# Issuing the combinations of a tile of weights behind the last low part of the tile two ahead of it

## The chip, the cores and the metric

The kernel runs on one core of a Trainium2 chip. What counts is the device time of one execution in microseconds. Times of this kernel are told as the median of several runs, and a profile is one execution of its own, taken by the hardware profiler.

## The reference

One layer of a hybrid block on 512 positions of width 2048, in float32. All of it hangs on large products with weights: one input projection of 22,592 columns, two branch projections and an output projection.

```python
h = rmsnorm(x, norm1_w[l])
proj = jnp.einsum('bsd,de->bse', h, w_in[l])
q, k, v, g_ret, z, xbc, dt_raw, gate_r, gate_s = jnp.split(proj, offsets, axis=-1)
y_r = (retention(q, k, v, positions) * jax.nn.silu(g_ret)).astype(x.dtype)
y_s = ssd(xbc, dt_raw, conv_w[l], conv_b[l], dt_bias[l], a_log[l], d_skip[l])
y_s = rmsnorm((y_s * jax.nn.silu(z)).astype(x.dtype), ssd_norm_w[l])
p_r = jnp.einsum('bse,ed->bsd', y_r, w_br_ret[l])
p_s = jnp.einsum('bse,ed->bsd', y_s, w_br_ssd[l])
merged = jax.nn.sigmoid(gate_r) * p_r + jax.nn.sigmoid(gate_s) * p_s
x = x + jnp.einsum('bsd,de->bse', merged, w_out[l])
return rmsnorm(x, norm_f_w)
```

`retention` has 8 heads of 256 with rotary q and k and a recurrence over chunks of 64; `ssd` is a causal depthwise convolution with a chunked scan over 64 heads in 8 groups. The second branch is 4096 wide, so its projection has twice the rows of the others.

## The kernel before

**The products.** A *unit* computes 256 output columns for all 512 positions: a contraction over 2048 rows in eight steps k of 256 rows. Each step is a 2 x 2 block product (two halves of 128 weight rows and columns, two halves of 256 positions). Most units do it with seven block products in place of eight, by Strassen's scheme (table `SEVEN`); some, called plain, do it with the four weight blocks against all 512 positions (`FOUR`). Float32 accuracy comes from splitting each operand into a high part, rounded to the type that TensorE takes, and a low part, what is left: each block product is three matmuls (high x high, high x low, low x high: lines 221 to 223), so a step is 7 x 3 = 21 matmuls of 256 columns.

**A tile of weights** (`wf`) holds two steps. SP loads it in two DMAs (four where a unit takes its columns from two places). For a Strassen unit VectorE (DVE) then adds the *combinations*, three instructions (lines 238, 240 and 241). Then, for each of the two steps, ScalarE (ACT) casts the seven blocks to the high part `whi` (line 148) and DVE subtracts it from them to make the low part `wlo` (line 149). There are three `wf` buffers, seven of `whi` and six of `wlo`, so the load of a tile waits until the last low part of the tile three back has been made.

**PSUM.** A unit's seven sums go to four buffers, pb0 to pb3 (halves of 256 positions). When they are complete, ACT copies pb0 (line 274) and DVE adds up pb1 (275), pb2 (276 and 277) and pb3 (278) into `o`. In the rotary heads and the SSD groups every unit uses the same four buffers, so the next unit's products can write pb2 only after line 277; in the branch and output projections units alternate between these and the four `att` buffers. The last three steps of a unit (`LAST`) run table group by table group, so that pb0 and pb1 are complete first.

**The stages.** Eight retention heads; eight SSD groups (each with units for B and C, x, z and the gates, and between them the convolution, the decays and the scan); the projection of the retention branch; that of the SSD branch in two halves of 2048 rows, called here the second and third branch projection; the output projection. Between these four the normalized activations are loaded (tiles `r`) and split: a difference, high and low part (lines 173, 174, 176) for the first four operands, and, while the first unit runs, three more (lines 182 to 187). In the third branch projection each unit also loads three tiles `f` a row block, multiplies and adds them (lines 737 on POOL, 738 to 740 on DVE), and stores the result for the output projection to load.

**What sets the order.** No order is written out, but for start and end. A scheduler simulates the program on a model of the engines and lists each engine's instructions; what is ready and has the higher priority goes first, and loads, combinations and parts have a raised priority (`tc.high_priority(offset=PRIO)`). Each engine then works through its list in order, and so does SP's queue of DMAs. `tc.add_manual_dep` with the class `NoSync` tells the scheduler that one instruction must stand behind another on its engine; it adds no semaphore.

## Time and profile before

| | us |
|---|---|
| median of 3 runs (lowest, highest) | 2753.27 (2751.96, 2756.13) |
| the profiled execution, its own time | 2755.9 |
| its span, first to last instruction | 2754.0 |
| TensorE busy | 2691.5 |
| VectorE busy | 2368.3 |
| ScalarE busy | 1342.7 |

The mean granted TensorE clock of that execution is 0.993 of full speed. In the views, PE is TensorE's matmuls, PEld its weight loads (which overlap them), DVE VectorE, ACT ScalarE, POOL GpSimd, SP the engine that issues most DMAs; L149 is line 149. A row of the waits reads: the engine that waited and the line of the instruction, what ended the wait, total us, times, the longest. A row of the time line: start, duration, engine, line, operation, tiles, and in brackets the idle time ahead of it and what ended it. A row of the windows: the stretch, its length, busy time of PE, PEld, DVE, ACT and POOL with the number of instructions, the granted clock, the share of the DMA engines, GB/s. The grouped rows: line, engine, operation, tiles, shapes, count, then busy us and mean ns, then idle time ahead and what ended it.

### The profile page before, as it was taken

To read this page: it belongs to the slowest core of one execution; us is meant where nothing else is said; L and a number is where in the kernel's file an instruction comes from. 1 tells how busy PE (TensorE), PEld (TensorE's weight loads), DVE (VectorE), ACT (ScalarE), POOL (GpSimd) and SP (SyncE) were. 2 spreads that over 40 slices of the span, in tenths; PEclk is the share of its full clock that TensorE was granted. 3 is DMA by queue.
4 is the path that set the end of the run, shared out by engine and by line. 5 is a ranking of instruction groups with operands and counts; after the bars stand their busy time and mean duration, and the time that the engine had idled before them with its cause. 6 is when DMAs were issued, how large, how long until landed. Compare 5 with 4: busy or idle time off the path is not lost.

```text
span 2754.0 us, 51975 instructions
## 1 busy us (share of the span) xinstructions
PE 2691.5 (98%) x20448; PEld 2565.0 (93%) x20448; DVE 2368.3 (86%) x3799; ACT 1342.7 (49%) x1923; POOL 179.3 (7%) x130
## 2 busy tenths in 40 slices
PE   7999999999999999999999999999999999999998
PEld 4899999999999999999999999999999999898897
DVE  7998888888869898888989898898989897898997
ACT  4434333433345555565565555566564353433443
POOL 0000000000000000000000000000000000011221
PEclk9999999999999999999999999999999999999999
DMA  4223333333333444343444434343464644557534
GB/s 156 85 89 108 100 104 104 104 93 104 104 113 121 129 129 129 107 129 114 131 127 134 138 107 125 119 136 121 129 202 154 212 140 131 176 182 226 193 120 138
DMA packets 339766, 362.46 MB, mean 132 GB/s; under 512 B 25152, under 2 KB 297792, under 8 KB 339520
## 3 DMA queue, kind: packets, MB, share of 16 engines
q1 hardware_dynamic: 319136, 325.05, 38.2%
q10 hardware_dynamic: 20384, 34.09, 3.3%
q8 instruction: 160, 2.62, 0.4%
q14 instruction: 86, 0.70, 0.1%
HBM read 321.56 MB, written 37.49 MB: 130 GB/s over the span
## 4 chain that ended last, share of the span: by engine, by line
PE 78%; DVE 9%; DMA 6%; issue 3%; ACT 1%; SPq 1%; POOL 0%; DVEq 0%; ACTq 0%; POOLq 0%
PE pb L223 21%; PE pb L221 21%; PE pb L222 21%; DMA wf<-in_w_in_dram 3%; DVE wlo L149 3%; PE att L222 2%; PE att L223 2%; PE att L221 2%; PE att L545 1%; DVE wf L238 1%; PE att L560 1%; PE att L677 1%; DMA wf<-in_w_br_ssd_dram 1%; PE att L681 1%; PE pb L118 1%
## 5 line engine op out<-in xcount | busy, mean ns | idle before, releaser
L148 ACT CAST whi<-wf 128x896 fp32r<-128x896 f32 (+1 forms) x968 | 817.6, 884 | 908.2 <-PE pb L222 370.4
L149 DVE TENSOR_TENSOR wlo<-wf,whi 128x896 fp32r<-128x896 f32 (+1 forms) x968 | 988.3, 1033 | 57.2 <-ACT whi L148 35.6
L221 PE MATMUL pb<-a,whi 128*128 128x256 f32 (+1 forms) x3328 | 998.3, 303 | 7.7 <-DVE o L277 4.3
L223 PE MATMUL pb<-a,wlo 128*128 128x256 f32 (+1 forms) x3328 | 994.5, 301 | 7.2 <-DVE wlo L149 7.1
L222 PE MATMUL pb<-a,whi 128*128 128x256 f32 (+1 forms) x3328 | 996.8, 300 | 0.0
L221 PEld LDWEIGHTS pb<-a,whi 128*128 128x128 f32 x3328 | 636.0, 191 | 32.3 <-issue 7.4
L223 PEld LDWEIGHTS pb<-a,wlo 128*128 128x128 f32 x3328 | 635.2, 191 | 30.4 <-DVE wlo L149 8.9
L222 PEld LDWEIGHTS pb<-a,whi 128*128 128x128 f32 x3328 | 637.1, 191 | 20.3 <-issue 0.2
L221 PE MATMUL pb<-b,whi 128*128 128x256 f32 x2112 | 600.1, 284 | 0.0
L223 PE MATMUL pb<-b,wlo 128*128 128x256 f32 x2112 | 599.0, 284 | 0.0
L222 PE MATMUL pb<-b,whi 128*128 128x256 f32 x2112 | 598.1, 284 | 0.0
L238 DVE TENSOR_TENSOR wf<-wf 128x512 f32<-128x512 f32 x400 | 286.1, 715 | 173.9 <-DMA wf<-in_w_in_dram 133.0
L221 PEld LDWEIGHTS pb<-b,whi 128*128 128x128 f32 x2112 | 405.8, 192 | 0.1
L222 PEld LDWEIGHTS pb<-b,whi 128*128 128x128 f32 x2112 | 405.8, 192 | 0.0
L223 PEld LDWEIGHTS pb<-b,wlo 128*128 128x128 f32 x2112 | 405.5, 192 | 0.2
L241 DVE TENSOR_TENSOR wf<-wf 128x256 f32<-128x256 f32 x400 | 174.9, 437 | 3.2
L240 DVE TENSOR_TENSOR wf<-wf 128x256 f32<-128x256 f32 x400 | 174.3, 436 | 3.5
L223 PE MATMUL att<-a,wlo 128*128 128x256 f32 (+1 forms) x480 | 144.5, 306 | 5.1 <-DVE wlo L149 5.1
L221 PE MATMUL att<-a,whi 128*128 128x256 f32 (+1 forms) x480 | 145.2, 305 | 0.0
L222 PE MATMUL att<-a,whi 128*128 128x256 f32 (+1 forms) x480 | 145.2, 305 | 0.0
L223 PEld LDWEIGHTS att<-a,wlo 128*128 128x128 f32 x480 | 90.8, 192 | 10.3 <-DVE wlo L149 6.5
L221 PEld LDWEIGHTS att<-a,whi 128*128 128x128 f32 x480 | 92.0, 192 | 3.9
(217 smaller groups left out, 2731.5 us busy)
## 6 DMA issues: line engine op xcount, KB each, us to landing
wf<-in_w_in_dram SPq DMA_DIRECT2D x640, 256.0 KB, 3.1
wf<-in_w_br_ssd_dram SPq DMA_DIRECT2D x128, 256.0 KB, 3.3
wf<-in_w_out_dram SPq DMA_DIRECT2D x72, 256.0 KB, 3.1
wf<-in_w_in_dram SPq DMA_DIRECT2D x128, 128.0 KB, 2.6
L<-A_d SPq DMA_DIRECT2D x32, 512.0 KB, 3.7
wf<-in_w_br_ret_dram SPq DMA_DIRECT2D x64, 256.0 KB, 3.4
ys_d<-B ACTq DMA_DIRECT2D x32, 256.0 KB, 2.0
r<-ys_d SPq DMA_DIRECT2D x16, 512.0 KB, 6.6
```

Source lines behind the costliest of these rows:

```text
L118: ins = getattr(self.engine, name)(*args, **kw).ins
L148: ACT.copy(dst_hi, src)
L149: DVE.tensor_tensor(dst_lo, src, dst_hi.bitcast(F32), op=ALU.subtract)
L221: PE.matmul(o, wh, xh, start=b not in started, stop=False, skip_group_check=True)
L222: PE.matmul(o, wh, xl, start=False, stop=False, skip_group_check=True)
L223: PE.matmul(o, wl, xh, start=False, stop=(k == NP - 1), skip_group_check=True)
L238: DVE.tensor_tensor(f2[:, :, 4:6, :], f2[:, :, 1:3, :], f2[:, :, 0:1, :].to_broadcast([P, 2, 2, P]), op=ALU.subtract)
L240: DVE.tensor_tensor(f2[:, :, 0, :], f2[:, :, 2, :], f2[:, :, 4, :], op=ALU.add)
L241: DVE.tensor_tensor(f2[:, :, 6, :], f2[:, :, 3, :], f2[:, :, 0, :], op=ALU.subtract)
L545: PE.matmul(ps[:, :n], k[:, i, sb * P:(sb + 1) * P], q[:, i, sb * P:], start=(i == 0), stop=(i == 1))
L560: PE.matmul(ps[:, :DK], pt[sb][:, (lb - sb) * P:(lb - sb + 1) * P], v[:, sb, :], start=(sb == 0), stop=(sb == lb))
L677: PE.matmul(pi[i * 64:(i + 1) * 64, c * P:(c + 1) * P], xd[:, c, i, :], L[:, i, c, :], start=True, stop=True)
```

## The change

`split` returns the name of the subtraction that makes the low part, and `products` keeps these names in a list. When the combinations of a tile are written, the first of them is told to stand, on DVE, behind the third-last name: the second low part of the tile two ahead of it. Plain units have no combinations and are unchanged, though their low parts are in the list.

```diff
--- before.py
+++ after.py
@@ -146,7 +146,16 @@
 
     def split(dst_hi, dst_lo, src):
         ACT.copy(dst_hi, src)
-        DVE.tensor_tensor(dst_lo, src, dst_hi.bitcast(F32), op=ALU.subtract)
+        return DVE.tensor_tensor(dst_lo, src, dst_hi.bitcast(F32), op=ALU.subtract).ins.name
+
+    lows = []
+
+    def behind(ins, other):
+
+        tc.add_manual_dep(
+            ins, other,
+            mybir.DependencyInfo(mybir.DependencyClass.NoSync, mybir.DependencyReason.DATA),
+            reason="order of issue")
 
 
 
@@ -235,14 +244,17 @@
                             SP.dma_start(out=v[:, :, c:c + w], in_=rows(ap, k + m))
                             c += w
                     if not plain:
-                        DVE.tensor_tensor(f2[:, :, 4:6, :], f2[:, :, 1:3, :],
-                                          f2[:, :, 0:1, :].to_broadcast([P, 2, 2, P]), op=ALU.subtract)
+                        first = DVE.tensor_tensor(f2[:, :, 4:6, :], f2[:, :, 1:3, :],
+                                                  f2[:, :, 0:1, :].to_broadcast([P, 2, 2, P]), op=ALU.subtract)
+
+                        if len(lows) > 2:
+                            behind(first.ins, lows[-3])
                         DVE.tensor_tensor(f2[:, :, 0, :], f2[:, :, 2, :], f2[:, :, 4, :], op=ALU.add)
                         DVE.tensor_tensor(f2[:, :, 6, :], f2[:, :, 3, :], f2[:, :, 0, :], op=ALU.subtract)
                 f = f2[:, k % 2]
                 hi = wp.tile([P, 7, P], F32R, name="whi", bufs=HB)
                 lo = wp.tile([P, 7, P], F32R, name="wlo", bufs=LB)
-                split(hi[:, :n, :], lo[:, :n, :], f[:, :n, :])
+                lows.append(split(hi[:, :n, :], lo[:, :n, :], f[:, :n, :]))
             ws.append((hi, lo))
             if k < NP - LAST:
                 for g in groups:
```

The lines behind the first new one move by 9 and, behind the second, by 12: lines 221 to 223 become 230 to 232, 238, 240, 241 become 247, 252, 253, and 275 to 278 become 287 to 290.

Since the scheduler simulates the whole program, the orders of DVE, PE, ACT and SP change in many places. On DVE the same instructions stand in another order. Before, the first combination of 199 of the 400 tiles with combinations stood ahead of the last low part of the tile two back; after the change, of none. On ACT, 13 loads of an activation table at line 672 are gone.

**Place 1: the end of a unit in an SSD group, on DVE** (`wf_13224`, `wf_13280`, `wf_13315` are three tiles in a row, each with two low parts, of which those of `wf_13224` are `wlo_13231` and `wlo_13256`; `o_13148` is the unit whose sums are added up). Before:

```order
L149 TENSOR_TENSOR wlo_13231<-wf_13224,whi_13230 128x896
L240 TENSOR_TENSOR wf_13280<-wf_13280 128x2x128
L241 TENSOR_TENSOR wf_13280<-wf_13280 128x2x128
L238 TENSOR_TENSOR wf_13315<-wf_13315 128x2x256
L275 TENSOR_TENSOR o_13148<-pb1_12921,o_13148 128x512
L240 TENSOR_TENSOR wf_13315<-wf_13315 128x2x128
L241 TENSOR_TENSOR wf_13315<-wf_13315 128x2x128
L276 TENSOR_TENSOR o_13148<-o_13148,pb2_12922 128x2x256
L149 TENSOR_TENSOR wlo_13256<-wf_13224,whi_13255 128x896
L277 TENSOR_TENSOR o_13148<-o_13148,pb2_12922 128x256
L149 TENSOR_TENSOR wlo_13287<-wf_13280,whi_13286 128x896
L278 TENSOR_TENSOR o_13148<-pb3_12923,o_13148 128x2x256
```

and now:

```order
L252 TENSOR_TENSOR wf_13280<-wf_13280 128x2x128
L253 TENSOR_TENSOR wf_13280<-wf_13280 128x2x128
L287 TENSOR_TENSOR o_13148<-pb1_12921,o_13148 128x512
L149 TENSOR_TENSOR wlo_13231<-wf_13224,whi_13230 128x896
L288 TENSOR_TENSOR o_13148<-o_13148,pb2_12922 128x2x256
L149 TENSOR_TENSOR wlo_13256<-wf_13224,whi_13255 128x896
L247 TENSOR_TENSOR wf_13315<-wf_13315 128x2x256
L289 TENSOR_TENSOR o_13148<-o_13148,pb2_12922 128x256
L149 TENSOR_TENSOR wlo_13287<-wf_13280,whi_13286 128x896
L149 TENSOR_TENSOR wlo_13312<-wf_13280,whi_13311 128x896
L252 TENSOR_TENSOR wf_13315<-wf_13315 128x2x128
L290 TENSOR_TENSOR o_13148<-pb3_12923,o_13148 128x2x256
```

The first combination of `wf_13315` stood ahead of all four sums and of `wlo_13256`; it now stands behind both low parts of `wf_13224`. The first sum (275, now 287) no longer has `wlo_13231` ahead of it, and the last one (278, now 290) has `wlo_13312` ahead of it as well.

On PE, the start of the unit that follows (pb2 is the buffer that line 277 frees). Before, and now:

```order
L223 MATMUL pb0_13164<-a2_211,wlo_13231 128x256
L221 MATMUL pb1_13165<-a2_211,whi_13230 128x256
L221 MATMUL pb2_13166<-a0_200,whi_13174 128x256
L222 MATMUL pb2_13166<-a0_200,whi_13174 128x256
L223 MATMUL pb2_13166<-a0_200,wlo_13175 128x256
```

```order
L232 MATMUL pb0_13164<-a2_211,wlo_13231 128x256
L230 MATMUL pb1_13165<-a2_211,whi_13230 128x256
L231 MATMUL pb1_13165<-a2_211,whi_13230 128x256
L232 MATMUL pb1_13165<-a2_211,wlo_13231 128x256
L230 MATMUL pb1_13165<-b2_429,whi_13230 128x256
L231 MATMUL pb1_13165<-b2_429,whi_13230 128x256
L232 MATMUL pb1_13165<-b2_429,wlo_13231 128x256
L230 MATMUL pb2_13166<-a0_200,whi_13174 128x256
```

The third step's products for pb1 now all stand ahead of the first product for pb2, five matmuls more. The first product for pb3 comes as the 55th matmul of the unit in place of the 37th.

**Place 2: the seventh unit of the third branch projection, on DVE** (`wf_28433` and `wf_28468` are its last two tiles with their low parts `wlo_28440`, `wlo_28465` and `wlo_28475`, `wlo_28479`; `r0`, `r1` and so on are the operands loaded for the output projection). Before:

```order
L278 TENSOR_TENSOR o_28289<-att_28064,o_28289 128x2x256
L173 TENSOR_TENSOR r0_28743<-r0_28743 128x256
L241 TENSOR_TENSOR wf_28468<-wf_28468 128x2x128
L738 TENSOR_TENSOR f_28295<-f_28295,o_28289 128x512
L738 TENSOR_TENSOR f_28306<-f_28306,o_28289 128x512
L149 TENSOR_TENSOR wlo_28440<-wf_28433,whi_28439 128x896
L149 TENSOR_TENSOR wlo_28465<-wf_28433,whi_28464 128x896
L739 TENSOR_TENSOR f_28295<-f_28295,f_28297 128x512
L149 TENSOR_TENSOR wlo_28475<-wf_28468,whi_28474 128x896
L173 TENSOR_TENSOR r1_28749<-r1_28749 128x256
L149 TENSOR_TENSOR wlo_28479<-wf_28468,whi_28478 128x896
```

and now, in two pieces that follow each other:

```order
L247 TENSOR_TENSOR wf_28468<-wf_28468 128x2x256
L149 TENSOR_TENSOR wlo_28440<-wf_28433,whi_28439 128x896
L182 TENSOR_TENSOR r0_28743<-r0_28743 128x256
L750 TENSOR_TENSOR f_28295<-f_28295,o_28289 128x512
L149 TENSOR_TENSOR wlo_28465<-wf_28433,whi_28464 128x896
L750 TENSOR_TENSOR f_28306<-f_28306,o_28289 128x512
L252 TENSOR_TENSOR wf_28468<-wf_28468 128x2x128
```

```order
L182 TENSOR_TENSOR r1_28749<-r1_28749 128x256
L751 TENSOR_TENSOR f_28295<-f_28295,f_28297 128x512
L182 TENSOR_TENSOR r2_28755<-r2_28755 128x256
L253 TENSOR_TENSOR wf_28468<-wf_28468 128x2x128
L752 TENSOR_TENSOR f_28295<-f_28295,f_28299 128x512
L182 TENSOR_TENSOR r3_28761<-r3_28761 128x256
L149 TENSOR_TENSOR wlo_28475<-wf_28468,whi_28474 128x896
L149 TENSOR_TENSOR wlo_28479<-wf_28468,whi_28478 128x896
```

`wlo_28440` stands ahead of the difference on r0 where it stood behind; those on r1, r2 and r3 stand ahead of both low parts of `wf_28468`, where only r1 stood ahead of the second.

**Place 3: the start of the output projection, on DVE** (`wf_29008`, `wf_29064`, `wf_29120` are the first three tiles with combinations; `wlo_29015` is the first low part of the first). Before, and now:

```order
L238 TENSOR_TENSOR wf_29120<-wf_29120 128x2x256
L173 TENSOR_TENSOR r7_28573<-r7_28573 128x256
L182 TENSOR_TENSOR xo5_28801<-r0_28743 128x512
L182 TENSOR_TENSOR xo6_28802<-r1_28749 128x512
L241 TENSOR_TENSOR wf_29064<-wf_29064 128x2x128
L240 TENSOR_TENSOR wf_29120<-wf_29120 128x2x128
L149 TENSOR_TENSOR wlo_29015<-wf_29008,whi_29014 128x896
```

```order
L253 TENSOR_TENSOR wf_29008<-wf_29008 128x2x128
L182 TENSOR_TENSOR r7_28573<-r7_28573 128x256
L191 TENSOR_TENSOR xo5_28801<-r0_28743 128x512
L191 TENSOR_TENSOR xo6_28802<-r1_28749 128x512
L253 TENSOR_TENSOR wf_29064<-wf_29064 128x2x128
L192 TENSOR_TENSOR xo5_28801<-r0_28743,xo5_28801 128x256
L149 TENSOR_TENSOR wlo_29015<-wf_29008,whi_29014 128x896
L192 TENSOR_TENSOR xo6_28802<-r1_28749,xo6_28802 128x256
L149 TENSOR_TENSOR wlo_29040<-wf_29008,whi_29039 128x896
L247 TENSOR_TENSOR wf_29120<-wf_29120 128x2x256
L185 TENSOR_TENSOR a7_28785<-r7_28573,a7_28785 128x1024
L149 TENSOR_TENSOR wlo_29071<-wf_29064,whi_29070 128x896
```

The combinations of `wf_29120` began ahead of that low part; they now begin behind both low parts of `wf_29008`.

## Prediction

> **What bounds the kernel now.** I read the page first, then the windows, then who waited for whom, then the time line at the worst places. The head of the page and its chain of waits:
>
> ```profile
> span 2754.0 us, 51975 instructions
> PE 2691.5 (98%) x20448; PEld 2565.0 (93%) x20448; DVE 2368.3 (86%) x3799; ACT 1342.7 (49%) x1923; POOL 179.3 (7%) x130
> PE 78%; DVE 9%; DMA 6%; issue 3%; ACT 1%; SPq 1%; POOL 0%; DVEq 0%; ACTq 0%; POOLq 0%
> ```
>
> TensorE stands idle for only 2754.0 - 2691.5 = 62.5 us, so no edit on VectorE can bring more than that, and what the change can bring lies in the part of it for which TensorE waits on VectorE. The windows show where it lies (rotary heads, SSD groups, first two branch projections, third branch projection, start of the output projection):
>
> ```profile
> 120.00:790.00 670.00, 667.05 (x5283) 649.39 (x5282) 569.42 (x993) 255.13 (x330) 22.57 (x30) 1.00 0.33 101
> 790.00:2080.00 1290.00, 1277.74 (x9961) 1224.22 (x9960) 1117.76 (x1760) 752.58 (x1151) 87.63 (x65) 1.00 0.42 129
> 2080.00:2390.00 310.00, 310.00 (x2295) 297.00 (x2295) 259.98 (x403) 130.54 (x169) 2.05 (x1) 1.00 0.51 168
> 2390.00:2545.00 155.00, 144.09 (x1088) 138.52 (x1088) 140.01 (x213) 54.73 (x72) 18.32 (x11) 0.98 0.60 193
> 2585.00:2612.00 27.00, 22.53 (x148) 21.20 (x149) 27.00 (x43) 13.90 (x19) 10.36 (x1) 0.87 0.39 132
> ```
>
> The columns are length, then busy time of PE, PEld, DVE, ACT and POOL. From 120 to 790 and from 2080 to 2390 TensorE loses 3 us and nothing. The loss sits in the SSD groups (12.3 us of 1290), the third branch projection (10.9 of 155) and the first units of the output projection (4.5 of 27). In the last two VectorE is busy 90% and 100%: there it is the bound, with TensorE waiting for it. Who ended TensorE's waits in these three windows, in that order:
>
> ```profile
> PE pb L221 <- DVE o L277: 4.3, 6, 1.7
> PE att L677 <- issue: 2.9, 3, 1.4
> PE pb L221 <- DVE o L275: 0.7, 2, 0.5
> ...
> PE pb L223 <- DVE wlo L149: 5.7, 3, 4.1
> PE att L223 <- DVE wlo L149: 5.1, 6, 1.9
> ...
> PE att L222 <- DVE b L187: 1.9, 1, 1.9
> PE att L221 <- ACT b L185: 1.7, 2, 1.1
> PE pb L223 <- DVE wlo L149: 0.9, 1, 0.9
> ```
>
> VectorE itself stands still for weights, over the whole run, at the first combination (line 238):
>
> ```profile
> DVE wf L238 <- DMA wf<-in_w_in_dram: 133.0, 157, 2.9
> DVE wf L238 <- DMA wf<-in_w_br_ssd_dram: 25.9, 21, 2.0
> ```
>
> That is 159 us in 178 waits, 0.89 us each, and nearly all of it costs nothing today: TensorE's waits for VectorE in the rows above are 18.6 us.
>
> **The change, part by part.** No instruction is added or taken away on DVE, PE, SP or POOL; the combinations move. Durations for what moves:
>
> ```profile
> L149 DVE TENSOR_TENSOR wlo<-wf,whi 128x896 fp32r<-128x896 f32 x800 | 872.2, 1100 | 46.7 <-ACT whi L148 31.8 <-PE pb L223 11.9 <-ACT yn L570 0.9
> L238 DVE TENSOR_TENSOR wf<-wf 128x512 f32<-128x512 f32 x400 | 286.1, 715 | 173.9 <-DMA wf<-in_w_in_dram 133.0 <-DMA wf<-in_w_br_ssd_dram 25.9 <-DMA wf<-in_w_br_ret_dram 8.4
> L240 DVE TENSOR_TENSOR wf<-wf 128x256 f32<-128x256 f32 x400 | 174.3, 436 | 3.5
> L241 DVE TENSOR_TENSOR wf<-wf 128x256 f32<-128x256 f32 x400 | 174.9, 437 | 3.2
> ```
>
> A tile of weights has three combinations (0.715 + 0.436 + 0.437 = 1.59 us) and two low parts (2.20 us). In the order before, the combinations of every second tile stand ahead of the last low part of the tile two back; now all stand behind it. A tile's load may start when the last low part of the tile three back has been made, so the move puts up to 2.20 us of other work between the start of that load and the instruction that needs it. Against the mean wait of 0.89 us this removes most of VectorE's waits. What it is worth goes stage by stage.
>
> *SSD groups (790 to 2080).* The unit at 1188 us, whose order stands in the part on the change:
>
> ```profile
> 1188.99 0.69 DVE L238 TENSOR_TENSOR wf<-wf 128x512 f32<-128x512 f32 x1 [0.97 <-DMA wf<-in_w_in_dram]
> 1191.69 0.69 DVE L238 TENSOR_TENSOR wf<-wf 128x512 f32<-128x512 f32 x1 [0.21 <-DMA wf<-in_w_in_dram]
> 1195.30 0.41 DVE L277 TENSOR_TENSOR o<-o,pb 128x256 f32<-128x256 f32 x1
> 1195.85 0.36 PE L221 MATMUL pb<-a,whi 128*128 128x256 f32 x1 [0.16 <-DVE o L277]
> ```
>
> Two waits for weights (1.18 us) stand ahead of the sums that free PSUM, and TensorE waits at their end. In the new order one low part (1.10) and one first combination (0.72) leave the place ahead of the first sum (L275): 1.8 us earlier. L277 has two third-size combinations less ahead of it (0.87 us earlier), and L278 has one low part and one combination more (1.10 + 0.44 - 0.87 = 0.67 us later). On PE the products that need pb2 stand 5 matmuls later and those that need pb3 18 later; at 0.12 us from start to start (14 matmuls in the PE rows below: 1.56 / 13) 0.6 and 2.2 us. So L277 gains 1.5 us against its user and L278 too (2.2 - 0.7). The other groups have this unit in the same order, so the waits on L277 and L275 (4.3 + 0.7) should go: I take 4 of the 5 us. From below: nothing, if VectorE, now earlier, only waits for TensorE's sums; from above 5.0 + 2.9, with the wait at line 677, which follows work on ACT and VectorE that comes earlier too.
>
> *Third branch projection (2390 to 2545).* VectorE's own waits there, and the worst place:
>
> ```profile
> DVE wf L238 <- DMA wf<-in_w_br_ssd_dram: 8.0, 8, 1.9
> DVE f L739 <- POOL f L737: 4.1, 3, 1.7
> DVE r L173 <- DMA r<-mm_d: 2.5, 1, 2.5
> ...
> 2524.26 0.28 PE L221 MATMUL pb<-a,whi 128*128 128x256 f32 x1
> 2525.82 0.28 PE L222 MATMUL pb<-a,whi 128*128 128x256 f32 x1
> 2530.24 0.80 PE L223 MATMUL pb<-a,wlo 128*128 128x256 f32 x2 [4.13 <-DVE wlo L149]
> ...
> 2531.00:2533.00 2.00, 2.00 (x12) 2.00 (x11) 2.00 (x4) 0.00 (x0) 0.00 (x0) 0.50 0.63 200
> 2533.00:2535.00 2.00, 2.00 (x11) 2.00 (x11) 2.00 (x4) 0.62 (x1) 0.00 (x0) 0.50 0.68 186
> ```
>
> VectorE's waits (14.6 us) and TensorE's (5.7 + 5.1 = 10.8) are two sides of one thing here. After the stall of 4.13 us the granted clock is 0.50 for two windows: 23 matmuls in 4 us, against 33 at 0.12 us; 10 x 0.12 = 1.2 us more. So 12 us can be won. The change moves two low parts ahead of the load of r that held up the wait of 4.13 us: one of the two that TensorE needs (wlo_28440) no longer stands behind the 2.5 us. But the loads of weights in this stage are late for another reason too:
>
> ```profile
> SPq L704 <- DMA mm_d<-f: 29.8, 11, 5.7
> 2516.10 0.42 SPq L704 DMA_DIRECT2D f<-m_d  x1
> 2522.33 0.34 SPq L704 DMA_DIRECT2D f<-ps_d  x1
> 2522.76 0.39 SPq L205 DMA_DIRECT2D r<-mm_d  x1
> 2524.26 1.44 SPq L205 DMA_DIRECT2D r<-mm_d  x3
> ```
>
> SP, in order, holds the loads of weights behind a load of f that waits for a store, up to 5.7 us, and no move of combinations shortens that. So I take half of the 8.0 us, 4 us, and leave the clock's 1.2 us and the r's as they are. From above 8.0 + 1.2 + 2.5 = 11.7; from below a loss, the second rival.
>
> The Trainium skill (TensorE: Matmul & The Clock Gate, What's actually happening) says that TensorE falls to half clock after an idle window of about 3.4 us. The trace agrees on the stall of 4.13 us and not on the window from 2585 on: no single wait there is over 1.9 us, and the mean clock is 0.87. By the page the sum would be 1.2 us lower if this stall stays under 3.4 us; by the second row a shorter stall among others may keep the clock low, and I leave it out.
>
> *Output projection (2585 to 2612).* Before, two of the three combinations of the third tile (`wf_29120`) stand ahead of the first low part there; now none does: 0.715 + 0.436 = 1.15 us of work leaves that place and comes back behind the first low parts. TensorE's waits are 4.5 us. I take a third, 1.5; bounds 0 and 8 (with the clock of 0.87, 13% of 27 us).
>
> *What the move costs.* Combinations that come later make the high part (ACT) later, and the low part of the same tile waits for it. The nearest row is the 31.8 us in 800 that low parts wait for ACT today (the row of line 149). From below it costs nothing; if that doubles, VectorE loses 32 us over the run, hidden where TensorE has work ahead of it (it loses nothing from 2080 to 2390, with VectorE 84% busy) and open in the 155 + 27 us that VectorE bounds, 182 / 2754 of it: 2 us. Elsewhere the cover is the buffers: six low tiles, so that a low part late by under a tile's 5 us (42 matmuls) is not felt.
>
> The sum: -4 - 4 - 1.5 + 2 = -7.5 us. The profiled execution has a span of 2754.0 and a time of 2755.9, 1.9 around it; the median is 2753.27, 2.6 below that time. 2753.27 - 7.5 is **2745.8; I say 2745.5 us**.
>
> **The rivals.**
> 1. *TensorE bound, nothing moves (16%).* Only 18.6 of TensorE's 62.5 idle us hang on VectorE at all, and a wait for weights that goes may come back as a wait for a buffer that TensorE has yet to free. For it: 159 us of waits today that almost nobody feels. Against it: in the two late windows they are felt. Then 4 us or less are won: 2749 to 2753.
> 2. *The loads of r decide (slower, 12%).* In the new order the sums on r1, r2 and r3 (line 173 before) stand ahead of both last low parts of the seventh unit of the third projection (wlo_28475, wlo_28479); before, only r1 stood ahead of the second. Their loads were issued from 2524.26 on; that of r0, issued at 2522.76, was waited for until 2527.22, 4.5 us, on a busy queue. If r3 lands 5 us after VectorE gets to it, TensorE waits those 5 us and runs at half clock behind them (1.2), ACT's 2 us come on top, and the SSD groups give only 2: +6.2, 2759.5. It decides once r3 is over 4 us late.
> 3. *All waits go (8%).* Then 5 + 2.9 + 11.7 + 4.5 = 24 us: 2729.
> 4. *The chip doesn't see the order (2%).* The added dependence binds the order of issue alone; but VectorE's order does change, so this is nearly excluded: 2753.
>
> ```profile
> 2527.22 0.42 DVE L173 TENSOR_TENSOR r<-r 128x256 f32<-128x256 f32 x1 [2.46 <-DMA r<-mm_d]
> ```
>
> **How the numbers follow.** My forecast has 62%. A change of 0.2% is 5.5 us, about what this kernel's measurement tells from none (its three runs span 4.2). Faster by more than that: five sixths of my forecast (52%), since the order shows nearly every sum that frees PSUM gaining on its user, and rival 3: 60%. Within 0.2%: the rest of the forecast (10%), rivals 1 and 4: 28%. Slower: rival 2, 12%. The range reaches halfway to rival 3 below, and above over rival 1 and most of the way to rival 2: 2733 to 2757.
>
> **What would show it.** Right: DVE's waits at the first combination fall from 159 us to under 80; TensorE's waits on L277 and L275 between 790 and 2080 fall under 1.5 us; PE idle in the 155 us of the third projection falls from 10.9 to about 7. The clock's dip at 2531 tells whether the longest stall stayed over 3.4 us. Wrong: these waits fall and the span stays (rival 1), or a wait of PE on wlo of 4 us and more stands right behind line 173 with r1 to r3 (rival 2).

## Result, and the profile after

The changed kernel takes 2719.95 us (median of 4 runs, 2718.35 to 2726.01), the kernel before, beside it, 2754.7 (2751.96 to 2757.35): a ratio of 0.9888, 95% interval 0.9875 to 0.9901, which is 27 to 34 us of 2754.7 (the medians differ by 34.8). In a repeat on the chip of some of the experiments (e10 below) it was 2720.52 against 2748.46: 0.9897 (0.9882 to 0.9912), 28 us less. The forecast was 2745.5, the range 2733 to 2757. So the sign was right, and the size wrong by a factor of about four. The time is below the range, and even below the case in which all waits go (2729).

The head of the page of the changed kernel, and its chain of waits:

```profile
span 2716.6 us, 51947 instructions
PE 2675.3 (98%) x20448; PEld 2558.6 (94%) x20448; DVE 2351.0 (87%) x3799; ACT 1326.7 (49%) x1910; POOL 191.2 (7%) x130
PE 88%; DVE 5%; DMA 4%; issue 2%; ACT 0%; SPq 0%; POOL 0%; DVEq 0%; ACTq 0%; POOLq 0%
```

VectorE's share of the chain falls from 9% to 5%, that of the DMAs from 6% to 4%; TensorE's rises from 78% to 88%. Its idle time is 2716.6 - 2675.3 = 41.3 us (62.5 before). The span fell by 37.4 us, the idle time by 21.2 only. The rest stood inside "busy", for two reasons at least. A matmul's row is 0.28 us long while the next usually starts after 0.12, so the first 0.16 us of every stall counts as busy (69 stalls before, 33 after: by estimate 6 us), and a matmul at half clock counts as busy for its whole length. In what follows a *stall* is a matmul that starts more than 0.22 us later than usual for its shape.

The same stretches of work as in the prediction's windows (their ends are set where TensorE starts the same matmul; columns as before):

```profile
118.00:786.00 668.00, 665.86 (x5278) 648.60 (x5277) 563.25 (x988) 254.90 (x328) 18.76 (x29) 1.00 0.34 101
786.00:2056.00 1270.00, 1270.00 (x9961) 1221.96 (x9960) 1108.78 (x1765) 735.61 (x1137) 102.52 (x66) 1.00 0.43 131
2056.00:2366.00 310.00, 310.00 (x2296) 297.01 (x2295) 262.58 (x408) 135.02 (x174) 1.29 (x1) 1.00 0.53 170
2366.00:2510.00 144.00, 140.80 (x1092) 136.63 (x1091) 135.56 (x205) 51.21 (x67) 19.66 (x11) 1.00 0.63 200
2549.00:2575.00 26.00, 22.23 (x152) 21.09 (x151) 25.15 (x41) 12.31 (x17) 6.78 (x1) 0.87 0.46 158
```

The SSD groups take 1270 us in place of 1290 and in this view TensorE is busy all through them; the third branch projection takes 144 in place of 155; the start of the output projection 26 in place of 27. VectorE's groups, low parts and first combinations (line 247, before 238):

```profile
L149 DVE TENSOR_TENSOR wlo<-wf,whi 128x896 fp32r<-128x896 f32 (+1 forms) x968 | 978.5, 1028 | 81.1 <-PE pb L232 48.4 <-ACT whi L148 18.4 <-ACT B L702 3.6
L247 DVE TENSOR_TENSOR wf<-wf 128x512 f32<-128x512 f32 x400 | 292.7, 732 | 46.3 <-DMA wf<-in_w_in_dram 27.4 <-DMA wf<-in_w_br_ssd_dram 7.7 <-DMA wf<-in_w_br_ret_dram 7.5
```

The idle time ahead of the first combinations falls from 173.9 to 46.3 us. What VectorE waits for now is mostly TensorE: 48.4 us for buffers ahead of low parts, 39.4 and 29.1 us for complete sums ahead of lines 288 and 287. It is ahead. Who ended TensorE's waits: in the SSD groups no row at all; in the third branch projection, then the two longest at the start of the output projection:

```profile
PE pb L230 <- ACT whi L148: 1.5, 2, 1.1
PE pb L232 <- DVE wlo L149: 0.9, 1, 0.9
PE att L232 <- DVE wlo L149: 0.8, 1, 0.8
...
PE att L231 <- DVE b L196: 1.8, 1, 1.8
PE att L230 <- ACT b L194: 0.8, 1, 0.8
```

Place 1 on VectorE's time line, the unit that stood at 1188 us before:

```profile
1177.55 0.68 DVE L287 TENSOR_TENSOR o<-pb,o 128x512 f32<-128x512 f32 x1
1178.15 1.08 DVE L149 TENSOR_TENSOR wlo<-wf,whi 128x896 fp32r<-128x896 f32 x1
...
1180.96 0.68 DVE L247 TENSOR_TENSOR wf<-wf 128x512 f32<-128x512 f32 x1
1181.56 0.41 DVE L289 TENSOR_TENSOR o<-o,pb 128x256 f32<-128x256 f32 x1
```

The first combination at 1180.96 waits for nothing; its counterpart had stood still 0.21 us ahead of the first sum, and the one ahead of that 0.97 us. Place 2, on VectorE and, behind the dots, on TensorE:

```profile
2492.37 1.08 DVE L149 TENSOR_TENSOR wlo<-wf,whi 128x896 fp32r<-128x896 f32 x1
2493.38 0.41 DVE L182 TENSOR_TENSOR r<-r 128x256 f32<-128x256 f32 x1
2498.85 0.43 DVE L182 TENSOR_TENSOR r<-r 128x256 f32<-128x256 f32 x1 [1.59 <-DMA r<-mm_d]
...
2490.30 0.51 PE L232 MATMUL pb<-a,wlo 128*128 128x256 f32 x2 [0.86 <-DVE wlo L149]
2500.77 0.39 PE L230 MATMUL pb<-a,whi 128*128 128x256 f32 x1 [1.09 <-ACT whi L148]
```

The low part at 2492.37 stands ahead of the first difference on an r (r0), which no longer waits; a later one waits 1.59 us. The stall of 4.13 us is gone; what TensorE waits for at 2500.77 is a high part of ACT.

That r0 doesn't wait has a cause in SP's list, which the change rearranged too:

```profile
2484.48 0.42 SPq L716 DMA_DIRECT2D f<-m_d  x1
2485.32 0.37 SPq L214 DMA_DIRECT2D r<-mm_d  x1
2489.74 0.33 SPq L716 DMA_DIRECT2D f<-ps_d  x1
```

Before, the load of r0 stood one place behind the load of f that waits for a store and was issued at 2522.76, 2.0 us before VectorE came to it at 2524.76. Now it stands one place ahead of it and is issued 8.1 us before VectorE comes to it.

### The profile page after: what moved, and what is told of

It reads as the page before. It is cut to its first block, busy times and chain, and to the rows that moved or that the text cites. A ratio compares the mean times of both kernels' runs of the same rounds, so it can differ in the third digit from the quotient of the medians.

```text
span 2716.6 us, 51947 instructions
## 1 busy us (share of the span) xinstructions
PE 2675.3 (98%) x20448; PEld 2558.6 (94%) x20448; DVE 2351.0 (87%) x3799; ACT 1326.7 (49%) x1910; POOL 191.2 (7%) x130
## 4 chain that ended last, share of the span: by engine, by line
PE 88%; DVE 5%; DMA 4%; issue 2%; ACT 0%; SPq 0%; POOL 0%; DVEq 0%; ACTq 0%; POOLq 0%
PE pb L230 24%; PE pb L232 24%; PE pb L231 24%; PE att L231 2%; PE att L230 2%; PE att L232 2%; DVE wlo L149 2%; PE att L572 1%; PE att L557 1%; PE att L689 1%; PE att L693 1%; PE pb L118 1%; DMA wf<-in_w_br_ssd_dram 1%; PE att L665 1%; DMA r<-ys_d 1%
## 5 line engine op out<-in xcount | busy, mean ns | idle before, releaser
L149 DVE TENSOR_TENSOR wlo<-wf,whi 128x896 fp32r<-128x896 f32 (+1 forms) x968 | 978.5, 1028 | 81.1 <-PE pb L232 48.4
L247 DVE TENSOR_TENSOR wf<-wf 128x512 f32<-128x512 f32 x400 | 292.7, 732 | 46.3 <-DMA wf<-in_w_in_dram 27.4
L253 DVE TENSOR_TENSOR wf<-wf 128x256 f32<-128x256 f32 x400 | 171.6, 429 | 2.5
L252 DVE TENSOR_TENSOR wf<-wf 128x256 f32<-128x256 f32 x400 | 169.7, 424 | 0.8
L286 ACT COPY o<-pb 128x256 f32<-128x256 f32 x88 | 32.7, 371 | 149.4 <-PE pb L232 149.3
L661 POOL TENSOR_TENSOR xl<-xd,sst 128x384 f32<-128x384 f32 x32 | 41.1, 1285 | 803.0 <-DVE xd L658 803.0
```

The source lines that it names most:

```text
L149: return DVE.tensor_tensor(dst_lo, src, dst_hi.bitcast(F32), op=ALU.subtract).ins.name
L247: first = DVE.tensor_tensor(f2[:, :, 4:6, :], f2[:, :, 1:3, :], f2[:, :, 0:1, :].to_broadcast([P, 2, 2, P]), op=ALU.subtract)
L252: DVE.tensor_tensor(f2[:, :, 0, :], f2[:, :, 2, :], f2[:, :, 4, :], op=ALU.add)
L253: DVE.tensor_tensor(f2[:, :, 6, :], f2[:, :, 3, :], f2[:, :, 0, :], op=ALU.subtract)
L286: ACT.copy(p1, pt[0][:, 0, :])
L661: POOL.tensor_tensor(xl, xd[:, :TB - 1], tail[:, :TB - 1, hs, None].to_broadcast([P, TB - 1, 2, 64]), op=ALU.mult)
```

## The experiments

What they have in common: a gain by stage is the difference between the traces in the time from one matmul's start to another's (the 1500th, 5754th, 15500th, 18000th, 19250th and 19420th of 20448). All are read against the one trace of the kernel before, whose execution was a long one (2755.9; on the four chips of the experiments its median is 2747 to 2750). So a stage that an experiment leaves untouched shows how far such a reading wanders: -1.1 to -2.5 us in the SSD groups (e2, e6, e7), -3.8 and -3.9 in the third projection (e1, e6), -1.6 to +0.2 up to the 1500th matmul where the order there is as before (e2, e6, e7) and -1.0 and -2.2 in repeats of the changed one (e13, e10). The medians, each against runs of the kernel before on the same chip, decide. e1 to e4 ran on one chip, e5 to e8, e9 to e12, and e13 and e14 on three others; where runs of different chips are compared, it is by what each gains against the kernel before.

| | median (against before) | ratio, 95% | SSD groups: gain, stalls | third projection: gain, stalls | ahead of first combinations |
|---|---|---|---|---|---|
| before | | | 15.7 (21) | 12.8 (11) | 173.9 |
| changed | -34.8 | 0.9875-0.9901 | -19.5, none | -12.0, 3.8 (4) | 46.3 |
| e1 until SSD | -16.3 | 0.9921-0.9959 | -19.5, none | -3.8, 9.4 (5) | 65.9 |
| e2 late only | -8.2 | 0.9964-0.9986 | -2.5, 13.1 (16) | -13.2, 2.6 (3) | 150.5 |
| e3 first low part | -18.1 | 0.9920-0.9956 | -15.9, 3.5 (7) | -10.2, 4.9 (7) | 144.4 |
| e4 four buffers | +16.4 | 1.0043-1.0077 | +21.5, 34.8 (41) | -15.5, 0.4 (1) | 228.6 |
| e5 old PE order | -21.9 | 0.9913-0.9942 | -15.6, 3.4 (4) | -11.4, 4.6 (4) | 47.7 |
| e6 new PE order | -0.8 | 0.9989-1.0008 | -2.2, 12.7 (22) | -3.9, 9.7 (8) | 174.8 |
| e7 r behind | -3.7 | 0.9980-0.9999 | -1.1, 14.7 (21) | -7.3, 7.7 (8) | 174.2 |
| e8 changed, four buffers | -21.4 | 0.9914-0.9947 | -13.3, 5.1 (7) | -12.2, 3.1 (3) | 0.0 |
| e9 no wait, old order | -27.8 | 0.9882-0.9912 | -17.9, 1.9 (1) | -12.2, 3.6 (3) | 0.0 |
| e10 changed again | -27.9 | 0.9882-0.9912 | -19.5, none | -11.4, 4.2 (3) | 51.0 |
| e11 between low parts | +103.8 | 1.0361-1.0396 | +72.8, 62.2 (85) | +1.9, 12.6 (14) | 0.0 |
| e12 behind low parts | +172.3 | 1.0606-1.0638 | +109.4, 92.8 (91) | +14.4, 23.1 (18) | 0.0 |
| e13 changed, r behind | -29.6 | 0.9881-0.9910 | -19.5, none | -9.1, 6.3 (7) | 51.7 |
| e14 changed, fewer parts | -31.4 | 0.9873-0.9906 | -19.2, 0.3 (1) | -13.9, 2.2 (3) | 44.7 |

All in us; in brackets behind stalls is their number; the last column is VectorE's idle time ahead of the first combinations over the run.

### e1 and e2: one part of the program each

```diff
-                        if len(lows) > 2:
+                        if ordered[0] and len(lows) > 2:
                             behind(first.ins, lows[-3])
...
+    ordered[0] = False      # e1; e2 starts with False and sets True here
     with tc.tile_pool(name="br", bufs=1) as bp:
```

e1: 

> The combinations are tied to the last low part of the tile two back only up to the end of the SSD groups; from the retention branch's projection on they stand where the scheduler puts them. Theory A (places on VectorE: in each stage by itself the waits of TensorE go because a first combination that waits for its weights no longer stands ahead of what TensorE needs; gains by stage in the changed kernel's trace, read at equal matmuls: 3.7 us up to 790 us, 20.2 in the SSD groups, 11.7 + 1.6 from the third branch projection on): 24 us less than before, some 2731 us, and the third branch projection with 10 us of TensorE idle as before. Theory B (the SSD gain is TensorE's other order and ACT's 13 fewer table loads): the same 24 us, since both are there as well. Theory C (the gain of the late stages hangs on what the early ones leave behind, as a phase of the DMA queues): the third branch projection gains here too, 2720 us.

e2: 

> The mirror image: tied only from the retention branch's projection on. Theory A: 13.3 us less than before, some 2741 us, with the SSD groups as before (TensorE idle 12 us of 1290). Theory C: the late gain is gone without the early one, within 4 us of before.

e1 gains 16 us, e2 8, together 24.5 of the 27.9 that the whole change brings in e10 (e1's interval alone is 10 us wide). The stalls in the SSD groups go in e1 and stay in e2; those of the third projection mostly the other way round (9.4 and 2.6 us left). So each stage gains by itself, as A says, and C falls. By the medians the late part is worth about 8 us rather than the 13 that the one trace of before suggested. In e1 the long stall of the third projection is still there, on TensorE behind an r that VectorE waits for (SP's list has its old order there), with the half clock behind it:

```profile
2499.64 0.42 DVE L182 TENSOR_TENSOR r<-r 128x256 f32<-128x256 f32 x1 [2.97 <-DMA r<-mm_d]
2502.71 0.80 PE L232 MATMUL pb<-a,wlo 128*128 128x256 f32 x2 [4.37 <-DVE wlo L149]
...
2500.00:2502.00 2.00, 0.00 (x0) 0.00 (x0) 2.00 (x5) 1.38 (x2) 0.00 (x0) 0.96 0.81 279
2502.00:2504.00 2.00, 1.29 (x6) 1.29 (x7) 2.00 (x3) 1.44 (x3) 0.00 (x0) 0.50 0.98 369
```

### e3: one low part less

```diff
-                        if len(lows) > 2:
-                            behind(first.ins, lows[-3])
+                        if len(lows) > 3:
+                            behind(first.ins, lows[-4])
```

> The first combination is tied to the first low part of the tile two back, not to the second: 194 of 400 still stand ahead of the second, but ACT has the 13 table loads less, as in the changed kernel. Theory A: one low part (1.1 us) in place of two lies between the start of a load and its user, so VectorE's waits for weights stay near 90 us (174 before, 46 after) and about half of the gain comes: 15 to 20 us less than before, 2735 to 2740. Theory B (table loads): all of the SSD gain of 20 us is there, whatever the waits for weights are.

18 us, with 144.4 us of waits for weights left in place of 46.3: A's estimate of the time is right and its reason is not, since the waits fell by a sixth, not by half. In the SSD groups alone most of the stalls went (3.5 of 15.7 us left). So the sum of VectorE's waits doesn't measure what they cost. I read it so that those cost which stand ahead of something that TensorE is waiting for; this run alone doesn't show that. Nor can it tell A from B: the table loads on ACT are gone here too (as in the changed kernel, 55 in place of 68). Two later runs do.

### e4 and e8: a fourth buffer, without the change and with it

```diff
-FB, HB, LB = 3, 7, 6
+FB, HB, LB = 4, 6, 5
```

e4 (on the kernel before): 

> The kernel before with its old order rule, four weight buffers in place of three (six high and five low tiles in place of seven and six, to make room): loads start a tile earlier, so the wait for weights goes without any rule on the combinations, 380 of 400 of which stand ahead of the last low part two back. Theory A: VectorE's waits for weights fall under 30 us and the gain is 20 us or more, unless the fewer high and low tiles cost some of it. Theory B (it is the place of the combinations itself or TensorE's order, not the wait): within 5 us of before.

e8 (on the changed kernel): 

> The changed kernel with four weight buffers (and six high, five low tiles). With four buffers alone the wait for weights had grown (from 174 to 228 us) and the SSD groups had lost 21 us, because the scheduler then put the combinations still further ahead. Theory A (the place counts, not the number of buffers): with the places tied, VectorE's waits for weights fall under 20 us, the SSD groups stay without stalls and the third projection gains as with four buffers alone (15 us): the changed kernel's time or up to 5 us less, 30 to 36 us less than before. Theory E (the SSD loss came from the fewer high and low tiles): the SSD groups lose 10 us or more against the changed kernel here too.

The same first combinations, of e4 and then of e8:

```profile
L238 DVE TENSOR_TENSOR wf<-wf 128x512 f32<-128x512 f32 x400 | 285.9, 715 | 228.6 <-DMA wf<-in_w_in_dram 195.8 <-DMA wf<-in_w_br_ssd_dram 22.0 <-DMA wf<-in_w_br_ret_dram 8.1
```

```profile
L247 DVE TENSOR_TENSOR wf<-wf 128x512 f32<-128x512 f32 x400 | 280.1, 700 | 0.0
```

My expectation of e4 failed: a buffer more made the waits longer. The scheduler lists an instruction when its simulated inputs are there; with four buffers it could list the combinations further ahead (380 of 400 stand ahead of the last low part of the tile two back, 199 with three), and on the chip the loads weren't there yet. The scheduler spent the room at once. How much of the 16 us is due to the fewer high and low tiles, no run tells: none has four weight buffers with seven and six of them. With the places tied, in e8, no first combination waits at all, and the same buffers are 38 us better (+16.4 and -21.4). Yet e8 is some 6 us behind the changed kernel, with 5.1 us of stalls back in the SSD groups. The fewer high and low tiles (E) cost nothing with three weight buffers (e14, below). Whether they do with four is open: low parts wait 66.5 us for ACT's high parts in e8, 37.5 in e14 and 18.4 in the changed kernel.

### e5 and e6: which engine's order does it?

```diff
+            book.extend(m.ins for m in (m1, m2, m3) if m is not None)
...
+    in_order_of(tc, book)
+    # ties each matmul of an SSD unit behind its predecessor in a list:
+    # e5, on the changed kernel: the list of the kernel before;
+    # e6, on the kernel before: the list of the changed kernel
```

e5: 

> The changed kernel, but the 8102 matmuls of the units of the SSD groups are tied into the order that they have before the change: VectorE keeps the new places of the combinations (all 400 behind), TensorE the old order. Theory A (VectorE's places): the SSD groups keep at least 15 of their 20 us, TensorE's stalls there under 4 us (15.7 us in 21 stalls before, by starts of matmuls more than 0.22 us late; none after the change), some 27 us or more less than before in all. Theory B (TensorE's order): the SSD gain falls to under 8 us, 15 to 20 us less than before in all.

e6: 

> The mirror image: the kernel before, 190 combinations ahead of the last low part two back, with the matmuls of the SSD groups tied into the order that they have after the change. Theory A: the SSD groups still stall (over 8 us of the 15.7), under 8 us less than before. Theory B: the SSD stalls go, 15 to 20 us less than before.

TensorE's new order on the old places brings nothing (-0.8 us); VectorE's new places with TensorE's old order bring 22 of 28 us, and 3.4 of the 15.7 us of stalls in the SSD groups are left. So the places on VectorE carry most of the gain, and the last few us go with TensorE's order once they are there (tying it also shifts some places on VectorE, ACT and SP, so this part isn't TensorE's alone for certain). e6 has 6 of the 13 table loads less as well and gains nothing: B falls for TensorE's order, and e9, below, has all the loads.

### e7 and e13: the loads of r

```diff
-        DVE.tensor_tensor(f[:, 4, :], f[:, 0, :], f[:, 1, :], op=ALU.subtract)
+        d = DVE.tensor_tensor(f[:, 4, :], f[:, 0, :], f[:, 1, :], op=ALU.subtract)
+        if last_r[0]:
+            tc.add_manual_dep(d.ins, last_r[0], ...)   # NoSync, as in behind()
...
+        last_r[0] = lows[-9]        # the last low part of the seventh unit
         load_operands(mm_d, NP - 1)
```

e7 (on the kernel before): 

> The kernel before; only the differences on the operands loaded for the output projection (r0 to r6) are tied behind the last low part of the seventh unit of the third branch projection. No combination moves elsewhere (19 of VectorE's places differ). Theory A (in the third projection about half of the 12 us is the one stall behind r0, 4.1 us, and the half clock behind it, 1.2 us): the stall of 4.1 us and the half clock go, 5 us less than before in that stage, the rest as before. Theory D (the gain there is the combinations' waits for weights, 8.0 us before, and the wait on r0 only takes the place of another): within 2 us of before in that stage.

e13 (on the changed kernel): 

> The changed kernel with e7's tie added: the differences on r0 to r6 stand behind the last low part of the seventh unit of the third projection. In the changed kernel's trace VectorE waits 1.6 us for one r ahead of that unit's last two low parts, and TensorE's stalls in the stage are 3.8 us in 4. If those still hang on the r's: 1.5 to 3 us less than the changed kernel. If not (the stalls left are ACT's high parts and the three combinations): the same within 1 us.

e7 gains 3.7 us with 19 of VectorE's places changed; the stage gains 7.3 in the trace, of which 3.8 is what an untouched one shows. So about 3.5 us of the late stages can be had from the one stall behind r0; the rest I put down to the combinations' waits (the interval, 0.3 to 5.5 us less, leaves room either way). SP's list has r0 in its old place here, so the new place of the differences does it by itself. The two parts don't simply add: e9, below, gains the stage's 12 us with 2.4 us of that stall left. In the changed kernel the tie adds nothing that intervals of 8 us would show (e13: -29.6 against -27.9 in e10): r0 no longer waits there, since SP issues its load earlier.

### e9: the old order without the waits

```diff
+                        fix = ident[:, None, None, :].to_broadcast([P, 2, 2, P])
-                        DVE.tensor_tensor(f2[:, :, 4:6, :], f2[:, :, 1:3, :],
-                                          f2[:, :, 0:1, :].to_broadcast([P, 2, 2, P]), op=ALU.subtract)
-                        DVE.tensor_tensor(f2[:, :, 0, :], f2[:, :, 2, :], f2[:, :, 4, :], op=ALU.add)
-                        DVE.tensor_tensor(f2[:, :, 6, :], f2[:, :, 3, :], f2[:, :, 0, :], op=ALU.subtract)
+                        DVE.tensor_tensor(f2[:, :, 4:6, :], fix, fix, op=ALU.subtract)
+                        DVE.tensor_tensor(f2[:, :, 5, :], fix[:, :, 0, :], f2[:, :, 4, :], op=ALU.add)
+                        DVE.tensor_tensor(f2[:, :, 6, :], fix[:, :, 0, :], f2[:, :, 5, :], op=ALU.subtract)
```

> The kernel before, with VectorE's and TensorE's instructions tied into the order that they have there (which is then the same on TensorE, VectorE and SP, and on ACT but for one pair that changes places). The three combinations of a tile keep their places, shapes and lengths, but read a constant tile in place of the loaded weights, so they wait for no load (ACT's cast then does; the combinations' values are left out of the computation). Theory W (the price of the old places is VectorE's standing still for weights there): TensorE's stalls in the SSD groups fall from 15.7 to under 4 us, and the whole to 15 us or more below before. Theory P (the price is the 1.59 us of work a tile that stands ahead of sums and low parts, waited for or not): the SSD stalls stay over 10 us, within 6 us of before.

2720.63 us: the changed kernel's time (e10: 2720.52, on the same chip in the same comparison), with the old order on every engine (but for the pair on ACT). Its first combinations, low parts, last combinations, and the SSD groups and third projection in windows:

```profile
L239 DVE TENSOR_TENSOR wf<-cc 128x512 f32<-128x512 f32 x400 | 284.0, 710 | 0.0
L149 DVE TENSOR_TENSOR wlo<-wf,whi 128x896 fp32r<-128x896 f32 (+1 forms) x968 | 989.1, 1032 | 95.0 <-ACT whi L148 36.2 <-PE pb L223 28.6 <-issue 12.0
L241 DVE TENSOR_TENSOR wf<-cc,wf 128x256 f32<-128x256 f32 x400 | 180.7, 452 | 3.3
...
786.00:2056.00 1270.00, 1268.23 (x9944) 1219.72 (x9943) 1117.32 (x1758) 753.52 (x1150) 86.25 (x64) 1.00 0.43 130
2366.00:2510.00 144.00, 141.58 (x1099) 137.89 (x1098) 133.58 (x208) 52.29 (x68) 25.90 (x11) 1.00 0.64 202
```

The combinations take about as long as before (710 and 452 ns, 715 and 437 before) and stand where they stood; only the standing still is gone, and with it 13.8 of the 15.7 us of stalls in the SSD groups and the same 12 us in the third projection as with the change. W holds, P falls: the work that stands ahead of the sums and low parts costs at most the 1.9 us of one stall there, the waiting costs the rest. ACT has all its table loads here (68, as before), so B is refuted a second time. The stall that is left is a matmul of the scan (line 623) that waits 1.8 us for ACT, 1.6 before.

### e10, e11, e12: the change again, and later still

```diff
-                            behind(first.ins, lows[-3])
+                            behind(first.ins, lows[-2])     # e11; e12: lows[-1]
```

e10: 

> The changed kernel once more, beside the other runs of this kernel on one chip. It was 1.1% faster than before elsewhere: 2717 us here, with no stall in the SSD groups and some 4 us in the third projection.

e11: 

> The combinations one step later: tied behind the first low part of the tile directly ahead (in the changed kernel: the second of the tile two ahead). The cast that follows them (0.88 us) still has one low part (1.1 us) beside it. If late combinations cost nothing as long as the cast is hidden: the changed kernel's time, within 5 us. If the lateness of the high part costs what I had put at 2 us or more (the low parts wait for ACT): 5 to 20 us above the changed kernel.

e12: 

> Later still: behind the second low part of the tile directly ahead. Nothing of the weights' own chain is then left on VectorE between a tile's combinations and its first low part, which waits for the cast: about 0.9 us a tile, 360 us over 400 tiles, against 386 us in which VectorE stands still before. VectorE becomes the bound in the SSD groups and from the third projection on: 20 to 80 us above the changed kernel. If sums and other work fill the gap: within 10 us of the changed kernel.

e10 came 3.5 us above what I expected. One low part later than in the changed kernel costs 132 us, two cost 200: neither of my two guesses for e11 comes near. The groups of e11:

```profile
L149 DVE TENSOR_TENSOR wlo<-wf,whi 128x896 fp32r<-128x896 f32 (+1 forms) x968 | 1004.2, 1043 | 276.4 <-ACT whi L148 250.3 <-PE pb L232 15.8 <-issue 5.6
L247 DVE TENSOR_TENSOR wf<-wf 128x512 f32<-128x512 f32 x400 | 274.9, 687 | 0.0
```

Nothing waits for weights any more, and low parts wait 250.3 us for ACT's high parts (18.4 in the changed kernel). That 0.88 us of cast beside 1.1 us of low part would hide it was wrong: the cast's wait is over only when all three combinations are done, and from then on to the low part there is nothing left in VectorE's list but what else is due. The low part that should have covered the cast stands ahead of the last combination:

```profile
1319.61 1.08 DVE L149 TENSOR_TENSOR wlo<-wf,whi 128x896 fp32r<-128x896 f32 x1
...
1321.06 0.43 DVE L253 TENSOR_TENSOR wf<-wf 128x256 f32<-128x256 f32 x1
1322.54 1.09 DVE L149 TENSOR_TENSOR wlo<-wf,whi 128x896 fp32r<-128x896 f32 x1 [1.05 <-ACT whi L148]
```

TensorE stalls in the SSD groups for 62.2 us in 85 places. The changed kernel's place is the last one ahead of this edge.

### e14: fewer high and low tiles

```diff
-FB, HB, LB = 3, 7, 6
+FB, HB, LB = 3, 6, 5
```

> The changed kernel with six high and five low tiles in place of seven and six, and three weight buffers. If the fewer tiles are what four buffers lost: the SSD groups lose about 6 us against the changed kernel (stalls of some 5 us), 5 to 10 us above it in all, since the third projection hasn't the fourth buffer either. If not: within 2 us of the changed kernel.

2718.18 us: no loss. With the combinations in their new places the kernel doesn't need the seventh high and the sixth low tile (7 KB a partition are free). The intervals of e10, e13 and e14 overlap, so no version beats the changed kernel measurably.

## Why the prediction was wrong, point by point

- **What bounds the kernel.** Held: nothing but time that TensorE loses was to be had. But 62.5 us is no measure of it. Some 20 us of that lie ahead of the first matmul and behind the last, and the first 0.16 us of each stall counts as busy: by starts the stalls over 0.22 us are 15.7 + 12.8 us in the two main stages where the windows had shown 12.3 + 10.9 idle.
- **SSD groups, -4: the step that failed.** Measured 19.5 us by the traces (e1, e10), 17 to 18.4 less the 1.1 to 2.5 of an untouched stage. The premise was that VectorE's 159 us of waits for weights cost almost nothing, because TensorE's rows that name VectorE come to 18.6 us. e9 takes these waits away, keeps the order, and gains 27.8 us. In this stage I took only the waits whose row named a sum on VectorE (L277 and L275, 5.0 us) and, as an upper bound, one more row (2.9, "issue"). The windows row quoted in the same text had 12.3 us idle, and another 3.4 us of its 21 stalls counted as busy. The rest stood in small rows of matmuls of the scan, which wait for ACT, VectorE and POOL (shown below). In e9 they are gone but for the first, so they hung on VectorE's standing still as well. As I read it, VectorE makes what the scan's matmuls and ACT use in the same list as the combinations, and a wait in it delays whatever stands behind, under the name of whoever is last.

```profile
PE att L623 <- ACT A L603: 1.6, 1, 1.6
PE att L681 <- DVE S L660: 1.1, 2, 0.6
PE att L653 <- POOL xl L649: 0.6, 1, 0.6
```

- **Third branch projection, -4.** 8 us by the medians (e2, all late stages), 12 in the one trace. I halved the waits for weights because SP holds loads behind a load of f, and left out the r and the half clock as unchanged. The waits fell about as foreseen (8.0 to 4.2 us), but the stall behind r0 went whole (e7 puts that at some 3.5 us). I had worked with SP's order of before, in which the load of r0 stands behind the load of f that waits for a store; the new list has it ahead, so r0 is there when VectorE comes to it.
- **Output projection, -1.5.** The trace has -1.3, but that is no support: e1 and e6, which leave this stage as it was, read -2.4 and -1.5.
- **Put at nothing.** Up to the 1500th matmul the trace has 3.7 us less; the repeats have 1.0 and 2.2, untouched runs up to 1.6, so it isn't told from noise.
- **The cost, +2.** Didn't appear: low parts' waits for ACT fell from 35.6 to 18.4 us. Why is open: they are 17.5 in e6, which gains nothing, and 36.2 in e9, which gains as much as the change. The danger that this term stands for is real and one step further on (e11: 250.3 us, +132).
- **The signs named.** Waits at the first combination under 80: 46.3. L277 and L275 under 1.5: no row. The third projection's idle time about 7: 3.2. The clock's dip at 2531: gone.
- **The rivals.** Of rival 1 the first half came true and the second didn't: waits turned into waits for TensorE, and the time fell all the same. Rival 2's order was there, but the r's came early enough (1.59 us, not 5). Rival 3, at 8%, came nearest, with too low a sum (24 us) for the same reason as the SSD term: it added up single rows in place of the stage's idle time. Its waits did not all go (46.3 us are left). The range's lower end, 2733, is three quarters of the way from the forecast to this rival, not half; half would be 2737. Rival 4 is excluded by e4 to e9.

## What to carry to other kernels

In this kernel a wait of an in-order engine was charged to everything behind it in its list, and the profile booked the damage on whoever was released last; bound what removing it can bring by the whole idle time of the stage (and by the starts of the matmuls, not their busy time), not by the rows that name the engine. A scheduler that places an instruction by a simulated landing of its load can spend a further buffer on placing it still earlier (e4); telling it where the instruction must stand is what kept the slack. How late is too late has an edge: one place further cost more than four times what the change had won (132 and 28 us), so the neighbouring places are worth a run each.

## What the runs showed of the hardware

TensorE's clock falls to half without any single long wait. In the changed kernel, at the start of the output projection (TensorE's waits, then two windows):

```profile
2557.32 0.62 PE L230 MATMUL att<-b,whi 128*128 128x256 f32 x3 [0.79 <-ACT b L194]
2559.39 0.38 PE L232 MATMUL att<-a,wlo 128*128 128x256 f32 x1 [0.74 <-DVE wlo L149]
2561.53 0.58 PE L231 MATMUL att<-b,whi 128*128 128x256 f32 x1 [1.75 <-DVE b L196]
...
2557.00:2561.00 4.00, 1.72 (x10) 1.32 (x10) 4.00 (x8) 1.10 (x2) 0.00 (x0) 0.90 0.11 38
2561.00:2565.00 4.00, 3.47 (x16) 3.47 (x17) 4.00 (x8) 2.86 (x4) 0.00 (x0) 0.50 0.29 93
```

Three waits of 0.74 to 1.75 us in some 5 us, TensorE busy 1.72 of 4, and the granted clock is 0.50 in the next 4 us (the mean of 0.90 puts the fall at about 2560.2 by estimate, inside the third wait). The Trainium skill (TensorE: Matmul & The Clock Gate, What's actually happening) tells of a window of about 3.4 us, free-running, in which activity is watched. One reading of it, that a wait must be that long, doesn't fit these rows; that short waits close together are enough does. So a row of several small stalls can cost a dip, which no row of the waits shows.

Nor did the dip behind the stall of 4.13 us, before the change, need the whole of it. That stall began at 2526.10:

```profile
2527.00:2529.00 2.00, 0.00 (x0) 0.00 (x0) 1.78 (x4) 0.86 (x2) 0.00 (x0) 0.83 1.05 391
2529.00:2531.00 2.00, 0.76 (x3) 0.77 (x4) 2.00 (x3) 1.97 (x4) 0.00 (x0) 0.50 1.05 397
```

A mean of 0.83, with 1.00 ahead and 0.50 behind, puts the fall at about 2528.3 by estimate, when TensorE had stood still for 2.2 us. The prediction's sign, that the dip tells whether this stall stayed over 3.4 us, doesn't hold by that.
